# A two-layer decoder trunk: the leftover pair of the Down projection moved to its front, its seven block products regrouped, and the residual centring moved to another engine

## The chip, the cores and the metric

The kernel runs on one core of one Trainium2 chip. The metric is the device time of one execution in microseconds (us). Before the change the median of 3 runs is 2747.27 us (2745.57 to 2750.97). Engines are named as in the profile: PE is the matrix engine, PEld its weight loads, DVE the vector engine, ACT the scalar engine, POOL the GpSimd engine, SP the engine that only issues transfers.

## What is computed

The input is one sequence of 1024 tokens with 1024 channels, in float32. Layer 0 mixes tokens with a state-space scan and a short gated convolution, layer 1 with sliding-window attention. After the mixer each layer does the same:

```python
def swiglu(x, w_gate, w_up, w_down):
    return (jax.nn.silu(x @ w_gate) * (x @ w_up)) @ w_down
...
x = layer_norm(ALPHA * x + mixer(x))
x = layer_norm(ALPHA * x + swiglu(x, ...))
x = x + (p[i] @ W_ple) * sigmoid(x @ W_gate + b_gate)
```

The hidden width is 2816, that is 22 slices of 128. The last line is called the PLE gate below; `p` has 256 channels.

## The kernel before

**Data.** Activations stand transposed: `r[m]` holds 128 channels (m = 0 to 7) by 1024 tokens, and a "half" H is 512 tokens. To keep float32 accuracy every operand is split into a high part (a rounding to the matmul type, made by a conversion on ACT) and a low part (the difference, made on DVE or POOL), and each product is three matmuls of 128x128 weights by 512 columns: high by high, high by low, low by high. A result block stands in one of eight PSUM banks of 128x512.

**Gate and up.** Slices 0 and 1 of the hidden width are done plainly and written to DRAM as `hC`. The other 20 slices go in 10 pairs, q = 0 to 9. In a pair, `seven` (L358) computes a 2x2 block product with seven instead of eight block products, for gate and then for up. From the pair's four blocks of h, the seven right-hand sides of the coming Down product are formed on DVE (`c`, `n`) and written to DRAM by SP as `hT[7, pair]` (L429). POOL adds the eight row blocks of x in `token_sum` (L402), from which the mean over channels is taken and written out as `xmd`.

**Down.** `ffn` does the 10 pairs in chunks of 4, 4 and 2 (L450). In a chunk it goes through seven products B11, B21, T2, T1, T3, B22, T4 (the loop at L552); a step is one product, and a kp inside it is two pairs, that is 24 matmuls. Each step needs weight combinations `wd`, made in `w8` (L509, L145, L502, L503) from raw weights `wr` by sums and differences in `left` (L541 to L546), and h tiles: loaded by POOL (`tf`, L393), split by ACT (`tt`, L470) and DVE (L471). Products accumulate in four banks `dx` or four banks `dy`. After every step four banks are added into `rr` (the result in SBUF), by ACT copies the first time (L490) and DVE additions after that (L488). In the second chunk the residual x is read back, centred on DVE (`rx` minus `xm`, L457) and added. After the chunks comes the **plain pair** (bank `dn`): hidden slices 0 and 1, from `hC`, 96 matmuls, eight banks per half. Behind each of its banks the statistics of the norm are gathered (`norm.add`), and `norm.finish(0)` (L216 is its reciprocal) writes the first half while the products of the PLE gate's first factor (`ple_products`) run.

**Column means.** All the weights of Down are centred. The means of their columns are taken early, while the input projection of layer 0 runs: 44 units, each a load of 512 KB by POOL (`dc`, L985) and one ACT instruction (L989), with three buffers and four units asked for after each half of a column block.

**Order.** Each engine works through its own list in order. The lists are made by a scheduler at build time, so they are read from the built program. Buffers come from pools; a tile that takes the place of another waits for the other's last reader, and that reader may be a transfer to DRAM.

Of the kernel before, what the change touches and what calls it, by code (L numbers as in the profile page):

```python
# [7 lines left out]
F32 = mybir.dt.float32  # L8
# [12 lines left out]
PLAG = 6  # L21
# [21 lines left out]
def trunk(ctx: ExitStack, tc: tile.TileContext, xT, pT, w_in, w_dt, w_out, w_q, w_k, w_v, w_o, w_gate, w_up, w_down,  # L43
# [118 lines left out]
    class Norm:  # L162
# [11 lines left out]
        def square(self, H, m):  # L174
            rm = self.r[m][:, hs(H)]
            if m == 0:
                self.q[H] = self.pool.tile([P, HB], F32, tag="lnq", name="lnq", bufs=2)
                A.activation(self.q[H], rm, AF.Square)
            else:
                sq = self.pool.tile([P, HB], F32, tag="lnt", name="lnt", bufs=2)  # L180
                A.activation(sq, rm, AF.Square)
                V.tensor_add(self.q[H], self.q[H], sq)
# [80 lines left out]
    def ffn_first(layer, X, tp, norm, extra):  # L263

        hC = tc.dram_tile([2, 2, P, HB], F32, name=f"hC{layer}")
        xmd = tc.dram_tile([2, P, HB], F32, name=f"xm{layer}")
# [7 lines left out]
        return w, hC, xmd, extra  # L274

    def ffn(layer, first, X, r, X2):
        w01, hC, xmd, (wq, cq) = first
        hT = tc.dram_tile([7, NPAIR, P, HB], F32, name=f"hT{layer}")
        xs = tc.dram_tile([KT, P, NT], F32, name=f"xs{layer}")
        c1 = ExitStack()  # L280
# [117 lines left out]
        def token_sum(q):  # L398

            acc, new = xsum[:, 0], xsum[:, 1]  # L400
            if 1 < q <= KT:
                G.tensor_add(acc, acc, new)  # L402
            if q < KT:
                nc.gpsimd.dma_start(new if q else acc, xs[q])
            elif q == KT:
                for H in range(2):
                    pm = bank("a", "xm")
                    T.matmul(pm, mean, acc[:, hs(H)], start=True, stop=True)
                    A.copy(new[:, hs(H)], pm)
                nc.gpsimd.dma_start(xmd.rearrange("h p n -> p h n"), new.rearrange("p (h n) -> p h n", h=2))  # L410

        for q in range(NPAIR):
# [3 lines left out]
            with tc.high_priority():  # L416
                A.activation(g1, g1, AF.Silu)
                A.activation(g2[:, h1], g2[:, h1], AF.Silu)
                A.activation(g2[:, h0], px, AF.Silu)
            u1, u2, px = seven(weights(w_up[layer, f], w_up[layer, f + 1]), "")  # L420
            if q == NPAIR - 1:
                early = [[load_t(hT[w, i:i + 2]) for i in (0, 2)] for w in (B11, B21)]
# [9 lines left out]
            token_sum(q)  # L432
# [14 lines left out]
        wraw = pool(c2, "wraw", bufs=4)  # L447
# [6 lines left out]
        def residuals(ms, rx, xm):  # L454
            for m in ms:
                t = rx.pop(0)
                V.tensor_sub(t, t, xm)  # L457
                stt(rr[m], t, ALPHA, rr[m], ALU.mult, ALU.add)

        turn = [0]  # L460

        def t8(name):
            i = turn[0] % 6
            turn[0] += 1
            return (fe if i < 2 else ft).tile([P, 2, 2, HB], F32R, tag="t", name=name, bufs=2 if i < 2 else 4)
# [10 lines left out]
        def new(j, H):  # L476
            if j % 2 == 0:
                x8[H] = wraw.tile([P, 2, 2, HB], F32R, tag="wr", name=f"x{j}{H}") if H == 1 and j >= 4 else t8(f"x{j}{H}")
# [5 lines left out]
        def add(m, H, ps):  # L484
            o = rr[m][:, hs(H)]
            with tc.high_priority():
                if (m, H) in touched:
                    V.tensor_tensor(out=o, in0=o, in1=ps, op=ALU.add)  # L488
                else:
                    A.copy(o, ps)  # L490
            touched.add((m, H))

        for ch, (q0, n) in enumerate(chunks):
            kps = range(n // 2)

            def w8(src, name, kp, which):
# [8 lines left out]
                for i in range(2):  # L505
                    f = 2 * (q0 + 2 * kp + i) + 2
                    c = NFF + f // 2 - 1 if which == T1 else f if which == B11 else f + 1
                    c = cen[:, layer, c:c + 1]
                    A.activation(w[:, 0, i], src[:, i], AF.Identity, bias=c)  # L509
                    stt(w[:, 1, i], src[:, i], c, w[:, 0, i].bitcast(F32), ALU.add, ALU.subtract)  # L510
# [13 lines left out]
            def raw_load():  # L524
                with tc.high_priority() if ch else ExitStack():
                    v = {}
                    for j in (0, 1) if ch else (1, 0):
                        for kp in kps:
                            t = wraw.tile([P, 2, KT, P], F32, tag="wr", name="wr")
# [5 lines left out]
            def left(kp, which):  # L535
# [3 lines left out]
                if which == T2:  # L539
# [4 lines left out]
                    return a11  # L544
                if which == B22:
                    V.tensor_sub(a12, a12, a11)  # L546
                return {T1: s1s[kp], T3: a21, B22: a12, T4: a22}[which]
# [4 lines left out]
            for step, which in enumerate((B11, B21, T2, T1, T3, B22, T4)):  # L552
                into_x = step % 2 == 0
                if step in (1, 3):
                    yb = [bank("a", f"dy{p}") for p in range(4)]
                bs = xb if into_x else yb
                fresh = step in (0, 1, 3)
                for kp in kps:
                    if step == 0 or step == 1 and ch:
                        W = direct(kp, step)  # L560
                    elif step == 1:
# [6 lines left out]
                    tt = split_t(early[step][kp] if ch == 0 and step < 2 else load_t(hT[which, q:q + 2]))  # L568
                    for i in range(2):
                        kk = 2 * kp + i  # L570
                        t = tt[:, i]
                        for p in range(4):
                            for j, (l, xl) in enumerate(((0, 0), (0, 1), (1, 0))):
                                T.matmul(bs[p], W[:, l, 4 * i + p, :], t[:, xl, :], start=fresh and kk == 0 and j == 0,  # L574
                                         stop=kk == n - 1 and j == 2, skip_group_check=True)
                if ch == 1:
                    residuals([[], [0], [1], [2], [3], [4, 5], [6, 7]][step], rx, xm)
                    for m in [[0], [1], [2], [3], [4, 5], [6, 7], []][step]:
                        rx.append(f4(xpool, "rx", "x"))
                        nc.gpsimd.dma_start(rx[-1], xs[m])  # L580
                elif ch == 0 and step == 6:
                    xm = f4(xpool, "xm", "x")
                    nc.gpsimd.dma_start(xm.rearrange("p (h n) -> p h n", h=2), xmd.rearrange("h p n -> p h n"))
                for p in range(4):
                    for m, H in {B11: [(0, 0)], B21: [(0, 0)], T2: [(0, 1)], T1: [(1, 1)], T3: [(1, 1)], B22: [(0, 1)], T4: [(1, 0)]}[which]:
                        add(2 * p + m, H, bs[p])
# [738 lines left out]
```

## Time and profile before

| | us |
|---|---|
| median of 3 runs | 2747.27 (2745.57 to 2750.97) |
| the profiled execution | 2751.04 |
| its span in the trace | 2749.3 |
| PE busy | 2650.7 (96%) |
| DVE busy | 1780.2 (65%) |
| ACT busy | 1134.5 (41%) |
| POOL busy | 436.8 (16%) |

The mean granted PE clock is 0.987 of full speed. The profiled execution is 3.8 us longer than the median. Matmuls are pipelined: one shows as 0.39 us long, though the next starts 0.23 us later, so the number of matmuls in a stretch tells more than PE's busy time. Layer 0's gate and up phase with `seven` runs from about 855 to 1244 us, its Down from 1244 to about 1507; layer 1's Down begins at about 2394.

### The profile page before, as it was taken

How to read it: one execution, taken by the hardware profiler on the slowest of the kernel's cores; microseconds unless marked ns; L12 is line 12 of the kernel's file. 1: busy time of each engine (PE TensorE's matmuls, PEld its weight loads, DVE VectorE, ACT ScalarE, POOL GpSimd, SP SyncE). 2: the span in 40 equal slices, each digit the busy share in tenths (PEclk: the TensorE clock that was granted, in tenths of full speed). 3: DMA queues.
4: the chain of work that ended last, by engine and by line, in shares of the span. 5: the costliest groups of instructions: out<-in, count | busy, mean ns of one | idle time of the engine just before them, and what ended most of it. 6: DMA issues, size and time to landing. Idle time of an engine off the chain costs nothing.

```text
span 2749.3 us, 31895 instructions
## 1 busy us (share of the span) xinstructions
PE 2650.7 (96%) x12234; PEld 2134.0 (78%) x12234; DVE 1780.2 (65%) x2763; ACT 1134.5 (41%) x1824; POOL 436.8 (16%) x387
## 2 busy tenths in 40 slices
PE   8999999999998999998999999999989999989999
PEld 6777777887876888886788887777778888867887
DVE  6787522274588666555897637775976556569873
ACT  5442362241244333333445546663533333343371
POOL 1111142111214100001121221001330000111122
PEclk9999999999999999999999999999999999989999
DMA  3100272311113323246543420002243233546332
GB/s 135 39 25 30 94 267 92 115 46 46 54 46 145 130 100 114 79 156 226 187 166 114 131 85 24 16 28 96 92 142 106 82 115 109 203 182 219 107 139 92
DMA packets 108697, 300.72 MB, mean 109 GB/s; under 512 B 10320, under 2 KB 27088, under 8 KB 108544
## 3 DMA queue, kind: packets, MB, share of 16 engines
q1 hardware_dynamic: 76624, 184.37, 19.4%
q0 software_dynamic: 31920, 114.31, 11.9%
q8 instruction: 96, 1.57, 0.2%
q14 instruction: 57, 0.47, 0.1%
HBM read 233.63 MB, written 65.01 MB: 109 GB/s over the span
## 4 chain that ended last, share of the span: by engine, by line
PE 77%; DVE 10%; issue 5%; ACT 4%; DMA 3%; POOL 1%; SPq 0%; POOLq 0%; ACTq 0%; DVEq 0%
PE px L358 16%; PE g L135 8%; PE g L136 8%; PE g L134 8%; PE pz L358 8%; PE pg L693 5%; PE dx L574 5%; PE dy L574 4%; PE py L358 4%; PE o L1152 2%; DMA hT<-c 1%; DVE tt L471 1%; PE pt L1143 1%; PE yd L944 1%; POOL dc L985 1%
## 5 line engine op out<-in xcount | busy, mean ns | idle before, releaser
L134 PE MATMUL g<-x,W 128*128 128x512 f32 x992 | 398.7, 402 | 13.3 <-ACT W L129 4.9
L135 PE MATMUL g<-x,W 128*128 128x512 f32 x992 | 396.9, 400 | 4.5 <-DVE x L112 2.6
L136 PE MATMUL g<-x,W 128*128 128x512 f32 x992 | 397.0, 400 | 2.5 <-POOL W L130 2.5
L130 POOL TENSOR_TENSOR W<-st,W 128x1024 fp32r<-128x1024 f32 x63 | 153.6, 2439 | 821.9 <-ACT W L129 821.7
L574 PE MATMUL dx<-tt,wd 128*128 128x512 f32 x960 | 228.3, 396 | 12.2 <-ACT tt L470 5.1
L134 PEld LDWEIGHTS g<-x,W 128*128 128x128 f32 x992 | 189.4, 191 | 57.6 <-ACT x L111 6.3
L358 PE MATMUL px<-T,wV 128*128 128x512 f32 x960 | 230.9, 389 | 1.5 <-DVE c L368 1.5
L135 PEld LDWEIGHTS g<-x,W 128*128 128x128 f32 x992 | 189.2, 191 | 49.1 <-DVE x L112 5.4
L574 PEld LDWEIGHTS dx<-tt,wd 128*128 128x128 f32 x960 | 182.9, 191 | 54.8 <-ACT tt L470 6.0
L136 PEld LDWEIGHTS g<-x,W 128*128 128x128 f32 x992 | 189.3, 191 | 43.9 <-POOL W L130 3.6
L358 PEld LDWEIGHTS px<-T,wV 128*128 128x128 f32 x960 | 180.0, 188 | 39.6 <-DVE c L368 2.3
L574 PE MATMUL dy<-tt,wd 128*128 128x512 f32 x720 | 181.0, 409 | 19.7 <-ACT wd L509 12.1
L129 ACT CAST W<-st 128x1024 fp32r<-128x1024 f32 (+1 forms) x97 | 100.5, 1040 | 209.8 <-PE g L136 145.5
L574 PEld LDWEIGHTS dy<-tt,wd 128*128 128x128 f32 x720 | 141.2, 198 | 56.0 <-ACT wd L509 13.8
L358 PE MATMUL px<-T,wS 128*128 128x512 f32 x480 | 118.2, 396 | 13.7 <-ACT c L368 13.7
L358 PEld LDWEIGHTS px<-T,wS 128*128 128x128 f32 x480 | 91.9, 192 | 33.8 <-ACT c L368 14.6
L470 ACT CAST tt<-tf 128x1024 fp32r<-128x1024 f32 x74 | 75.8, 1046 | 101.2 <-PE dx L574 42.4
L358 PE MATMUL px<-x,wA 128*128 128x512 f32 x480 | 116.2, 391 | 0.0
L471 DVE TENSOR_TENSOR tt<-tf,tt 128x1024 fp32r<-128x1024 f32 x74 | 89.0, 1220 | 41.0 <-ACT tt L470 40.8
L358 PE MATMUL pz<-T,wU 128*128 128x512 f32 x480 | 115.3, 389 | 0.0
L358 PE MATMUL pz<-x,wS 128*128 128x512 f32 x480 | 115.3, 389 | 0.0
L358 PE MATMUL py<-x,wA 128*128 128x512 f32 x480 | 115.3, 389 | 0.0
(318 smaller groups left out, 5289.4 us busy)
## 6 DMA issues: line engine op xcount, KB each, us to landing
tf<-hT POOLq DMA_DIRECT2D x70, 512.0 KB, 4.9
dc<-in_w_down POOLq DMA_DIRECT2D x44, 512.0 KB, 4.9
st<-in_w_gate SPq DMA_DIRECT2D x44, 512.0 KB, 3.2
st<-in_w_up SPq DMA_DIRECT2D x44, 512.0 KB, 4.2
st<-in_w_in SPq DMA_DIRECT2D x43, 512.0 KB, 3.2
hT<-n SPq DMA_DIRECT2D x40, 512.0 KB, 6.4
wr<-in_w_down SPq DMA_DIRECT2D x24, 512.0 KB, 5.4
hT<-c SPq DMA_DIRECT2D x20, 512.0 KB, 4.7
```

Of the source, the lines that this page charges most:

```text
L129: A.copy(W[:, 0, ks], st[:, ks])
L130: lo_eng[k % len(lo_eng)].tensor_sub(W[:, 1, ks], st[:, ks], W[:, 0, ks].bitcast(F32))
L134: T.matmul(ps, W[:, 0, i, :], X[:, 0, :], start=first, stop=False)
L135: T.matmul(ps, W[:, 0, i, :], X[:, 1, :], start=False, stop=False)
L136: T.matmul(ps, W[:, 1, i, :], X[:, 0, :], start=False, stop=last)
L358: T.matmul(ps, W[:, l, o + k, :], x[:, xl, :], start=first and k == 0 and j == 0, stop=k == 3 and j == 2, skip_group_check=True)
L470: A.copy(t[:, :, 0], st)
L471: V.tensor_sub(t[:, :, 1], st, t[:, :, 0].bitcast(F32))
L574: T.matmul(bs[p], W[:, l, 4 * i + p, :], t[:, xl, :], start=fresh and kk == 0 and j == 0, stop=kk == n - 1 and j == 2, skip_group_check=True)
L693: T.matmul(ps[:, c:c + n], W[m][l][:, i, :], X[i][H][:, xl, c:c + n], start=i == j == 0, stop=i == KT - 1 and j == 2)
L944: T.matmul(yd[64 * k:64 * k + 64, ci * P:(ci + 1) * P], xdt[:, ci, p * P + 64 * k:p * P + 64 * k + 64], M[:, k * 256 + ci * P:k * 256 + (c ...
L1152: T.matmul(ov[64 * hd:64 * hd + 64, bi * P:(bi + 1) * P], vt[:, b - 1 + kb, vc], pt[hd][:, 2 * bi + kb, :], start=kb == kbs[0], stop=kb == 1)
```

## The change

- **Plain pair first.** It moves from the end of Down to its start. Its sixteen banks are the first to touch `rr`, so they leave by ACT copies; all later ones are DVE additions. Its `hC` tiles and the four early `hT` tiles are loaded in the last up product.
- **Two chunks instead of three**, of 4 and 6 pairs: 28 bank additions of 128x512 fewer per layer.
- **Order in the last chunk**: B11, B21, T2, T3, T4, T1, B22, with T2, T3 and T4 following each other on the same four banks. The rows of the first half of the tokens are final after T4, and `norm.finish(0)` stands inside T1. The loop over the four banks is now outside the loop over the pairs of a kp, so banks end one after another.
- **Residual.** POOL subtracts the mean in the gate and up phase and writes the centred rows out (`xc`): eight more loads, subtractions of 128x1024 and writes per layer. DVE keeps only the scaled addition, now in chunk 0.
- **PLE gate.** Its inputs and weights are loaded in step B22, and all eight `ple_products` stand behind B22. The lag between the halves (`PLAG`) is 4 instead of 6.
- **Column means**: two buffers instead of three, and up to three units per half at three places instead of four at one.

```diff
-PLAG = 6
+PLAG = 4
...
+        token = token_steps()
...
+            for k in range(KT):
+                nc.gpsimd.dma_start(new, xs[k])
+                yield
+                G.tensor_sub(new, new, acc)
+                nc.gpsimd.dma_start(xc[k], new)
...
             if q == NPAIR - 1:
-                early = [[load_t(hT[w, i:i + 2]) for i in (0, 2)] for w in (B11, B21)]
+                hh = [load_t(hC[H]) for H in range(2)]
+                early = [load_t(hT[w, i:i + 2]) for w in (B11, B21) for i in (0, 2)]
...
-        chunks = [(0, 4), (4, 4), (8, 2)]
+        chunks = [(0, 4), (4, 6)]
...
+        hh = [split_t(t) for t in hh]
+        for H in range(2):
+            for m in range(MT):
+                ps = bank("a", "dn")
+                for i in range(2):
+                    mm3(ps, Wd[i], m, hh[H][:, i], i == 0, i == 1)
+                add(m, H, ps)
...
-            for step, which in enumerate((B11, B21, T2, T1, T3, B22, T4)):
+            for step, which in enumerate((B11, B21, T2, T3, T4, T1, B22) if end else (B11, B21, T2, T1, T3, B22, T4)):
...
+                    if end and which == T1 and kp == 1:
+                        norm.finish(0)
+                    for p in range(4):
+                        for i in range(2):
...
-                residuals([[], [0], [1], [2], [3], [4, 5], [6, 7]][step], rx, xm)
+                if ch == 0:
+                    for t, m in rx:
+                        stt(rr[m], t, ALPHA, rr[m], ALU.mult, ALU.add)
...
-            cp = pool(cctx, "cen", bufs=3, side="right")
+            cp = pool(cctx, "cen", bufs=2, side="right")
...
-                for _ in range(4) if j >= 2 else ():
+                if j >= 2:
                     next(cs, None)
```

Three places in the engines' lists show the move. The first is ACT at the start of layer 0's Down. A number behind a name is a tile's own; `tt` is a split h tile, `rr` the result, `dx` and `dn` banks, `W` and `wd` weights. Before:

```order
L470 CAST tt<-tf 128x2x512 x2
L509 ACTIVATE wd<-st,vec 128x512 x2
L509 ACTIVATE wd<-wr,vec 128x512 x2
L470 CAST tt<-tf 128x2x512 x2
L509 ACTIVATE wd<-wr,vec 128x512 x2
L490 COPY rr_8515<-dx_8523 128x512
L490 COPY rr_8517<-dx_8524 128x512
L490 COPY rr_8519<-dx_8525 128x512
L490 COPY rr_8521<-dx_8526 128x512
L509 ACTIVATE wd<-wr,vec 128x512 x2
```

And with the change:

```order
L477 CAST tt<-tf 128x2x512 x2
L506 ACTIVATE W<-st,vec 128x1024
L506 ACTIVATE wd<-st,vec 128x512 x2
L500 COPY rr_8542<-dn 128x512
L500 COPY rr_8543<-dn 128x512
L500 COPY rr_8544<-dn 128x512
L477 CAST tt<-tf 128x2x512 x2
L500 COPY rr_8545<-dn 128x512
L477 CAST tt<-tf 128x2x512
L500 COPY rr_8546<-dn 128x512
L500 COPY rr_8547<-dn 128x512
L500 COPY rr_8548<-dn 128x512
```

The first four copies of the plain pair's banks now stand ahead of the h tile that comes third for the seven products (the single `tt` row), and the other twelve copies behind it.

The second place is DVE there, where `s` and `wr` are the sums of raw weights in `left`, and the scaled addition with `rx` is one residual row. Before:

```order
L145 SCALAR_TENSOR_TENSOR wd<-wr,vec,wd 128x512 x2
L471 TENSOR_TENSOR tt<-tf,tt 128x2x512 x2
L145 SCALAR_TENSOR_TENSOR wd<-wr,vec,wd 128x512 x2
L541 TENSOR_TENSOR s_8685<-wr 128x1024
L542 TENSOR_TENSOR wr<-wr 128x8x128
L543 TENSOR_TENSOR wr<-s_8685,wr 128x8x128
L541 TENSOR_TENSOR s_8723<-wr 128x1024
L546 TENSOR_TENSOR wr<-wr 128x8x128
L542 TENSOR_TENSOR wr<-wr 128x8x128
L471 TENSOR_TENSOR tt<-tf,tt 128x2x512
```

And with the change:

```order
L478 TENSOR_TENSOR tt<-tf,tt 128x2x512 x4
L574 TENSOR_TENSOR s_8861<-wr 128x1024
L574 TENSOR_TENSOR s_8865<-wr 128x1024
L575 TENSOR_TENSOR wr<-wr 128x8x128 x2
L576 TENSOR_TENSOR wr<-s_8861,wr 128x8x128
L576 TENSOR_TENSOR wr<-s_8865,wr 128x8x128
L145 SCALAR_TENSOR_TENSOR rr_8543<-rx,rr_8543 128x1024
L145 SCALAR_TENSOR_TENSOR wd<-st,vec,wd 128x512 x2
L145 SCALAR_TENSOR_TENSOR wd<-wr,vec,wd 128x512
```

Four splits, six raw sums and a residual row now stand in one piece ahead of the low parts of the second weight tile of B11 (`wd<-st`).

The third place is ACT in the input projection, where `c` is the first column block of a half and `dc` a unit of the column means. Before:

```order
L1006 COPY c<-g 128x512
L989 ACTIVATE dc,vec<-dc 128x1024 x3
L129 CAST W<-st 128x1024
L1010 ACTIVATE ysc_2623<-spre,vec 128x512
L989 ACTIVATE dc,vec<-dc 128x1024 x3
L129 CAST W<-st 128x1024
L989 ACTIVATE dc,vec<-dc 128x1024 x3
L1006 COPY c<-g 128x512
```

And with the change:

```order
L1034 COPY c<-g 128x512
L1017 ACTIVATE dc,vec<-dc 128x1024 x2
L129 CAST W<-st 128x1024
L1042 ACTIVATE ysc_2623<-spre,vec 128x512
L1017 ACTIVATE dc,vec<-dc 128x1024 x2
L129 CAST W<-st 128x1024
L1017 ACTIVATE dc,vec<-dc 128x1024 x2
L1034 COPY c<-g 128x512
```

Between two copies `c` stood nine units and now stand six; over all, the 44 units lie in five halves before (8, 9, 10, 8, 9) and in seven now (6, 6, 8, 6, 8, 6, 4).

## Rows read from the trace of the kernel before

**Rows 1.** The page, busy time: engine, us, share of the span, instructions.
```profile
PE 2650.7 (96%) x12234; PEld 2134.0 (78%) x12234; DVE 1780.2 (65%) x2763; ACT 1134.5 (41%) x1824; POOL 436.8 (16%) x387
```

**Rows 2.** Windows: length, then busy us (instructions) per engine, PEclk, DMA share, GB/s.
```profile
930.00:1080.00 150.00, 150.00 (x664) 124.20 (x663) 90.67 (x115) 51.70 (x68) 0.00 (x0) 1.00 0.31 106
1250.00:1400.00 150.00, 134.84 (x552) 107.19 (x551) 112.51 (x124) 62.02 (x80) 23.41 (x35) 0.94 0.60 211
2400.00:2550.00 150.00, 134.25 (x542) 106.44 (x541) 114.54 (x126) 62.38 (x81) 23.20 (x34) 0.93 0.59 207
```

**Rows 3.** Waits of PE in layer 0's Down: us in total, times, longest.
```profile
PE dy L574 <- ACT wd L509: 6.3, 2, 4.0
PE dy L574 <- DVE wd L145: 2.7, 2, 1.8
PE dx L574 <- ACT tt L470: 2.6, 1, 2.6
```

**Rows 4.** Timeline of PE, first products of layer 0's Down: start, us, count, idle before.
```profile
1244.25 11.04 PE L574 MATMUL dx<-tt,wd 128*128 128x512 f32 x48
1255.13 5.60 PE L574 MATMUL dy<-tt,wd 128*128 128x512 f32 x24
1264.70 8.63 PE L574 MATMUL dy<-tt,wd 128*128 128x512 f32 x24 [3.97 <-ACT wd L509]
```

**Rows 5.** Timeline of ACT, same place: third conversion of an h tile.
```profile
1262.98 1.04 ACT L470 CAST tt<-tf 128x1024 fp32r<-128x1024 f32 x1 [16.25 <-DMA hT<-c]
```

**Rows 6.** DMA, 1225 to 1275: queues (packets, MB, share), then issues to landing.
```profile
q0 software_dynamic: 2448, 8.91, 48.7%
q1 hardware_dynamic: 5184, 3.93, 24.3%
...
tf<-hT POOLq DMA_DIRECT2D x9, 512.0 KB, 11.0
wr<-in_w_down POOLq DMA_DIRECT2D x8, 512.0 KB, 5.8
...
hT<-c SPq DMA_DIRECT2D x1, 256.0 KB, 17.3
```

**Rows 7.** Windows, six microseconds after the last up product.
```profile
1250.00:1256.00 6.00, 6.00 (x28) 4.99 (x27) 0.63 (x1) 0.00 (x0) 0.72 (x1) 1.00 1.04 395
```

**Rows 8.** Groups of DVE in layer 0's Down: count, busy, mean ns, idle.
```profile
L471 DVE TENSOR_TENSOR tt<-tf,tt 128x1024 fp32r<-128x1024 f32 x35 | 42.1, 1219 | 15.9 <-ACT tt L470 15.8
L488 DVE TENSOR_TENSOR rr<-rr,dx 128x512 f32<-128x512 f32 x36 | 23.4, 683 | 3.1 <-PE dx L574 3.1
...
L145 DVE SCALAR_TENSOR_TENSOR wd<-wr,vec,wd 128x512 fp32r<-128x512 f32 x24 | 17.3, 745 | 0.1
...
L457 DVE TENSOR_TENSOR rx<-rx,xm 128x1024 f32<-128x1024 f32 x8 | 9.5, 1218 | 0.0
```

**Rows 9.** Timeline of POOL and DVE, one such sum and DVE beside it.
```profile
899.98 2.61 POOL L402 TENSOR_TENSOR xsum<-xsum 128x1024 f32<-128x1024 f32 x1 [2.96 <-DMA xsum<-xs]
...
900.84 2.29 DVE L434 TENSOR_TENSOR n<-c 128x512 f32<-128x512 f32 x1
```

**Rows 10.** Windows, the stretch of all seven sums.
```profile
865.00:911.00 46.00, 45.36 (x194) 37.11 (x195) 31.71 (x34) 14.54 (x20) 20.92 (x13) 0.97 0.54 180
```

**Rows 11.** Windows, 100 us in which the column means are taken.
```profile
350.00:450.00 100.00, 92.56 (x395) 74.34 (x394) 24.29 (x39) 50.85 (x85) 35.42 (x38) 0.98 0.63 213
```

**Rows 12.** Windows of the column means' ACT instructions alone (two a unit), 100 us.
```profile
325.00:425.00 100.00, 49.63 (x87) 0.98 0.76 258
```

**Rows 13.** Timeline of ACT there: one column mean and its wait.
```profile
368.07 1.06 ACT L989 ACTIVATE dc<-dc 128x1024 f32<-128x1024 f32 x1 [3.58 <-DMA dc<-in_w_down]
```

**Rows 14.** The page, DMA issues: KB each, median us to landing.
```profile
dc<-in_w_down POOLq DMA_DIRECT2D x44, 512.0 KB, 4.9
```

**Rows 15.** Timeline of DVE, end of layer 0's Down and the norm behind it.
```profile
1505.28 1.30 DVE L488 TENSOR_TENSOR rr<-rr,dn 128x512 f32<-128x512 f32 x2
...
1538.93 0.69 DVE L112 TENSOR_TENSOR x<-rr,x 128x512 fp32r<-128x512 f32 x1
```

More of the change, by code (lines that the diff above doesn't have):

```diff
@@ L567, in ffn @@
                     q = q0 + 2 * kp
[L568 to L572, printed above, removed]
+                    tt = split_t(early.pop(0) if early else load_t(hT[which, q:q + 2]))
+                    if end and kp == kps[-1] and which in (T4, T1):
+                        w = {T4: T1, T1: B22}[which]
+                        early = [load_t(hT[w, q0 + 2 * i:q0 + 2 * i + 2]) for i in kps]
@@ L584, in ffn @@
+                e, H = reads[which]
                 for p in range(4):
-                    for m, H in {B11: [(0, 0)], B21: [(0, 0)], T2: [(0, 1)], T1: [(1, 1)], T3: [(1, 1)], B22: [(0, 1)], T4: [(1, 0)]}[which]:
-                        add(2 * p + m, H, bs[p])
-        loaded = ple_load(layer, wraw, t8)
-        hh = [split_t(load_t(hC[H])) for H in range(2)]
+                    add(2 * p + e, H, bs[p], end and which in (B21, T4, T1, B22))
         lo_eng[:] = [V]
-        Wd = []
-        for i in range(2):
-            with tc.high_priority():
-                st = spool.tile([P, KT, P], F32, tag="st", name="st")
-                nc.sync.dma_start(st, w_down[layer, i])
-                W = wpool.tile([P, 2, KT, P], F32R, tag="w", name="W")
-                c = cen[:, layer, i:i + 1]
-                A.activation(W[:, 0], st, AF.Identity, bias=c)
-                stt(W[:, 1], st, c, W[:, 0].bitcast(F32), ALU.add, ALU.subtract)
-            Wd.append(W)
@@ L602, in ffn @@
-        for H in range(2):
-            for m in range(MT):
-                ps = bank("a", "dn")
-                for i in range(2):
-                    mm3(ps, Wd[i], m, hh[H][:, i], i == 0, i == 1)
-                add(m, H, ps)
-                with tc.high_priority() if H == 0 else ExitStack():
-                    norm.add(H, m)
-            if H == 0:
-                ple_products(layer, *loaded, range(4))
-                norm.finish(0)
-                ple_products(layer, *loaded, range(4, MT))
-                wpools[:] = [wpool] * 3 + [As(wraw, "wr")] * 2
@@ L615, in ffn @@
-        return rr, c2, lnp, norm
+        wpools[:] = [wpool]
+        ple_products(layer, PX, Wp, range(MT))
+        return rr, c2, lnp, norm, As(wraw, "wr")
     class As:
@@ L674, in pieces, with weight @@
             return hi, lo
-        for m in range(4):
-            W[m] = pieces(m)
+        def weight(m):
+            if m in (3, 4):
+                W[m] = pieces(m)
+            else:
+                w = unit(w_pg[layer, m], at=more if m in (5, 6) else None)
+                W[m] = w[:, 0], w[:, 1]
+        for m in range(6):
+            weight(m)
         for m, H in lag_order(MT, PLAG):
@@ L680, in ple @@
                 norm.finish(1)
-            if H == 0 and m >= 4:
-                w = unit(w_pg[layer, m])
-                W[m] = w[:, 0], w[:, 1]
+            if H == 0 and 5 <= m < MT - 1:
+                weight(m + 1)
             pw = tp.tile([P, HB], F32, tag="pw", name="pwt", bufs=2)
@@ L1019, in trunk @@
         lo_eng[:] = [V, G]
+        for _ in cs:
+            pass
         cctx.close()
```

160 lines of the change are left out of this document (94 added, 66 removed).

## The prediction

> **What bounds the kernel now.** I read the busy times first. PE is busy 96% of the span, DVE 65% [rows 1], and the change leaves the number of matmuls as it is, so time can come only from stretches where PE does not run at its rate. I look for these in the windows. In a steady stretch 664 matmuls start in 150 us, 0.226 us each [rows 2]; that is the rate to measure against. In the first 150 us of layer 0's Down only 552 start: 112 are missing, 25.3 us. In layer 1's it is 542: 122 are missing, 27.6 us. So 52.9 us of the 2751.0 are lost at the start of the two Downs, which is what the change rebuilds.
>
> The waits of PE in layer 0's Down say for what: high parts of weights from ACT 6.3 us, low parts from DVE 2.7 us, the conversion of h tiles on ACT 2.6 us [rows 3]. PE's timeline has the place. It starts Down at 1244.25 and does 72 matmuls, then waits 3.97 us, and the 24 matmuls behind that wait take 8.63 us [rows 4], where 24 at the steady rate take 5.4: PE came back at its lower clock, 1.2 instead of 2.4 GHz, after the pause. ACT's timeline names the cause. The third conversion stood 16.25 us, until 1262.98, for the write `hT<-c` [rows 5]: its tile lies where that write still reads. And the write is late because of traffic: 256 KB took 17.3 us to land, while nine loads `tf` and eight `wr` of 512 KB were on the way [rows 6] and the transfer engines moved 395 GB/s at a share of 1.04 [rows 7], which is all they give here. So the last writes of h share the transfers with the first loads of Down, and PE has 72 matmuls, 16.3 us, to bridge that.
>
> **The change part by part.**
>
> *Plain pair first.* Its 96 matmuls are 21.8 us of PE work that need neither `hT` nor raw weights. The work is moved, not added; at its old place nothing waited on it. What it covers is the late write. But the write is still in the way: ACT's new list has four bank copies, then the conversion that waits for `hT<-c`, then the other copies. With eight banks and four emptied, PE can do 12 banks of 6 matmuls, 16.3 us. The write was issued about 1.3 us after the start of Down and takes 17.3 [rows 5, 6], so the conversion ends near 19.6 and PE stands up to 3.4 us. If the write lands as fast as the small loads (5.8 us) it stands 0. Ends 0 and 3.4; I take **2.0**, nearer to the row of the same transfer. The pause is then shorter than the 3.97 us after which PE fell to the lower clock.
>
> How fast such a write goes can be asked of the Trainium skill too: by its page "DMA: Bandwidth & Descriptors", section "Queues, rings and completion order", each transfer engine goes round between the queues it has work for, a packet at a time. With packets of 3.6 KB on POOL's queue and 0.76 KB on SP's (MB over packets), SP's queue would get 17% of 395 GB/s, an estimate of 68 GB/s; the 768 KB of both `c` writes [rows 6] would take 11.5 us and the stall be nil, which makes the total 4 us lower. The row has 17.3, and the row goes into the sum.
>
> *Behind it on DVE.* Four splits, six raw sums and a residual row now precede the low parts of B11's second weight tile. The last split can start when its conversion ends, at 19.6; it takes 1.22, the six sums and the residual 7 x 1.22, the two low parts 2 x 0.75 [rows 8], which gives 30.9. PE wants them after 21.8 + 5.4 + 2.0 = 29.2. Stall **1.6** (0 if the sums run while DVE waits for that split, 4 with another microsecond or two of transfer).
>
> *Chunk 0.* Its DVE list holds 14 splits (17.1), 28 low parts in 14 weight tiles (about 19), 8 raw sums (9.8), 8 residual rows (9.7) and 28 bank additions (19.1) [rows 8]: some 75 us beside 14 x 24 matmuls, 76 us. That fits, but the list is in order, and today DVE's low parts cost 2.7 us in a Down that is less full. **1.5** (0 to 4).
>
> *Fewer bank additions, centring away.* 28 additions of 0.683 and 8 subtractions of 1.218 per layer leave DVE, 28.9 us [rows 8]. They lie beside PE work, so they pay only by making room for the two terms above; I count nothing for them again. Behind the six-pair chunk's boundary and where T2, T3 and T4 follow each other on the same banks, a bank is free for an addition 1.36 us ahead of the next, and an addition takes 0.68. **1.5** (0 to 3).
>
> *Norm and last step.* `finish(0)` stands after one kp of T1, and the reciprocal and the sums of squares wait for the last additions of T4; in step B22 the conversions for the PLE gate stand ahead of one h tile. By the lengths on DVE and POOL (0.7 to 2.6 us each) [rows 8, 9], **2.3** (0 to 5).
>
> *PLE gate.* From the last bank addition (1506.58) to the last split of the second half (1539.62) pass 33 us [rows 15]. All `ple_products`, 21.8 us, and five products of 5.4 us now lie between: 49 us, enough for a lag of 4. **0.5** (0 to 2).
>
> So a Down would lose 2.0 + 1.6 + 1.5 + 1.5 + 2.3 + 0.5 = 9.4 us, both 18.8, against 52.9: a **gain of 34.1**. With all the low ends 0 is lost and with all the high ends 21.4 in each.
>
> *Centring on POOL.* Eight more subtractions per layer, near the sums' 2.61 us [rows 9], and 16 transfers of 512 KB, lie in gate and up, where PE runs full and transfers at a share of 0.31 [rows 2]. They are paced by pairs some 65 us apart. Nothing. What covers them is the 40% of DVE that is idle there: beside such a sum, a DVE subtraction took 2.29 us [rows 9] instead of 0.68. The Trainium skill, page "SBUF — State Buffer", section "SBUF: two separate sides", has the rule: DVE and POOL share one port pair, and whoever comes second waits out the other's whole instruction. The row agrees, and the rule speaks against this move; I price it as a rival.
>
> *Column means.* In the 100 us concerned 395 matmuls start [rows 11] of 442: 47 missing, 10.6 us. With three buffers nearly all of the 88 instructions of the 44 units lie in 100 us [rows 12], some 2.2 us a unit, 98 in all, against 81 us of PE work in their five halves (72 matmuls each): 17 us more, of which 10.6 show and banks bridge some 7. Two buffers give, per unit, half of (load + 1.06 + about 0.5 of turning round); with a load of 3.6 [rows 13] that is 2.6 us, with the median 4.9 [rows 14] 3.2 us. Over seven halves, 114 us of PE work, 44 units take 114 to 142 us, and banks bridge 7 again. The loss is thus 0 to 21 instead of 10.6: a gain of 10.6 or a loss of 10. Fewer loads at once should make each faster, so I lean to the lower end: a **gain of 3**.
>
> **Sum.** 2751.0 − 34.1 − 3 = 2713.9 for the profiled execution. The median lies 3.8 below that, and I keep **2714** for it, leaving those 4 us for waits that I did not find.
>
> **Rivals.**
>
> *The stall moves behind the pair.* If the write lands 5 us later than today, since two `hC` tiles are loaded as well, PE stands over 6 us, comes back at the lower clock (3.2 us for 24 matmuls) [rows 4], and DVE's list is as late: some 9 more per layer, **2732**. For it: the transfers are full [rows 7]. Against: `hC` is loaded a product earlier. 0.16.
>
> *Nearly all stalls go.* DVE's room swallows them: 4 lost per layer and 8 gained in the means, 2751 − 45 − 8 = **2698**. For it: the 28.9 us per layer. Against: in-order lists always leave some. 0.14.
>
> *POOL holds DVE up.* If each of 16 subtractions delays DVE by 1.6 us, as the sum in the row does [rows 9], and PE feels each, 26 us go, **2740**. Against: beside seven sums PE was busy 45.36 of 46 us [rows 10]. 0.04.
>
> *Slower: the column means become the bound.* With a unit at u us the loss is 44u − 121. It eats all of Down's gain when it passes 10.6 + 34, at u = 3.8, that is a load of 6 us with two under way. At 4.1 the loss is 59 and the time about **2762**. Against: the median load is 4.9 with three under way. 0.07.
>
> **How the numbers follow.** The forecast has 0.59, with its own bounds 2704 to 2724. Range 2697 to 2740: it leaves out the slower case and the tails of the others, some 0.15 to 0.2. A difference of 0.2%, 5.5 us, is about what a measurement can tell from none. Faster by more: forecast, both milder rivals and most of the POOL case, 0.88; within: 0.05; slower: 0.07.
>
> **What would show it.** In the windows of the changed kernel the first 150 us of each Down should hold 620 to 660 matmuls; in PE's timeline the pair should run 72 matmuls without a gap, then pause under 3.5 us, and no 24 matmuls behind take 8 us. In ACT's timeline the third h tile's conversion should still wait for `hT<-c`. Waits of PE for the means' copies should be fewer. I am wrong if either Down loses over 16 us, if the stretch of the means loses more than 15, or if gate and up fall below 664 matmuls in 150 us.

## The result and the profile after

The changed kernel takes 2716.47 us (median of 4 runs, 2714.06 to 2721.06), the kernel before 2749.12 beside it. The ratio is 0.9877, with a 95% interval of 0.9846 to 0.9908: 1.2% faster. The forecast of 2714 is 2.5 us off. The profiled execution's span fell by 37.1 us, from 2749.3 to 2712.2, and the sum had 37.1. But the parts do not match: several terms of the sum were wrong, and their errors cancel.

The busy times of the changed kernel answer to [rows 1]. POOL is busy 60 us more. DVE has 72 instructions less, 57.7 us at the lengths of [rows 8], yet it is busy only 18.7 us less: some 39 us went into other instructions that got longer.

```profile
PE 2636.0 (97%) x12234; PEld 2128.4 (78%) x12234; DVE 1761.5 (65%) x2691; ACT 1133.7 (42%) x1824; POOL 496.9 (18%) x431
```

The windows of the changed kernel (length, busy us and instructions per engine, PEclk, DMA share, GB/s) answer to [rows 2, 11]:

```profile
350.00:450.00 100.00, 93.91 (x398) 76.20 (x397) 21.95 (x38) 52.57 (x89) 37.76 (x43) 0.97 0.67 233
930.00:1080.00 150.00, 150.00 (x660) 123.50 (x659) 93.19 (x114) 51.28 (x68) 11.06 (x8) 1.00 0.35 123
1250.00:1400.00 150.00, 150.00 (x664) 124.20 (x663) 125.07 (x145) 68.01 (x90) 25.34 (x37) 1.00 0.65 227
1400.00:1500.00 100.00, 95.57 (x408) 77.32 (x407) 65.50 (x71) 58.02 (x83) 26.80 (x22) 0.98 0.32 112
2400.00:2550.00 150.00, 150.00 (x664) 124.20 (x663) 120.43 (x145) 63.58 (x81) 21.73 (x31) 1.00 0.52 178
2550.00:2650.00 100.00, 94.51 (x402) 76.14 (x401) 75.18 (x76) 63.59 (x92) 35.32 (x32) 0.98 0.36 126
```

Both Downs now begin at the full rate: 664 matmuls in the first 150 us, where 552 and 542 were [rows 2]. At 0.226 us each that gives 52.9 us back, all that was lost there. Gate and up hold 660, with eight POOL instructions that were not there. The four that are missing (0.9 us) are no loss to POOL: the mean's own four matmuls `xm` now stand in this window (1051.14), the only place in it where matmuls start late; before they stood at 1204.40, outside it. The column means have not improved: 398 matmuls, 395 before [rows 11]. And a new loss stands at the end of Down: 408 and 402 matmuls in the last 100 us. The same two windows of the kernel before:

```profile
1400.00:1500.00 100.00, 98.99 (x435) 81.27 (x434) 78.50 (x102) 48.78 (x70) 23.28 (x20) 1.00 0.29 103
2550.00:2650.00 100.00, 100.00 (x441) 82.44 (x440) 77.91 (x102) 50.40 (x73) 23.69 (x20) 1.00 0.28 99
```

That is 27 and 39 fewer, 14.9 us. So 52.9 − 14.9 = 38.0 us come from Down and next to nothing from elsewhere. PE's waits in layer 0's Down and the gate behind it (us in total, times, longest) name the new place; the three kinds of wait in [rows 3] had 11.6 us:

```profile
PE dy L619 <- DVE tt L478: 3.5, 2, 2.2
PE pg L721 <- DVE x L112: 1.2, 1, 1.2
PE dy L619 <- ACT tt L477: 1.0, 1, 1.0
```

How the start was emptied shows in four places of the changed kernel. SP's timeline, POOL's, ACT's, and the DMA issues between 1215 and 1265 us (KB each, us to landing):

```profile
1242.76 0.34 SPq L438 DMA_DIRECT2D hT<-c  x1
...
1245.27 0.72 SPq L438 DMA_DIRECT2D hT<-c  x1
```

```profile
1243.77 3.13 POOL L564 DMA_DIRECT2D wr<-in_w_down  x6 [6.39 <-PE px L358]
```

```profile
1250.44 1.06 ACT L477 CAST tt<-tf 128x1024 fp32r<-128x1024 f32 x1
```

```profile
hT<-c SPq DMA_DIRECT2D x1, 512.0 KB, 14.3
hT<-c SPq DMA_DIRECT2D x1, 256.0 KB, 2.0
```

The first write `hT<-c` goes out 1.0 us ahead of the last six raw loads and lands in 2.0 us. The same two issues before, of SP and POOL:

```profile
1245.60 1.58 SPq L429 DMA_DIRECT2D hT<-c  x2
```

```profile
1242.67 3.13 POOL L531 DMA_DIRECT2D wr<-in_w_down  x6 [4.33 <-PE px L358]
```

There the write went out three microseconds behind the first of those six loads and took 17.3 [rows 6]. Both ends moved: against the start of Down the write goes out 1.9 us earlier and the six loads 2.0 us later. The second write goes out behind them and takes 14.3. The third conversion of an h tile, which stood 16.25 us [rows 5], starts at 1250.44 without any wait. The chain behind it on DVE is early too; its low parts for B11's second pair:

```profile
1265.35 1.42 DVE L145 SCALAR_TENSOR_TENSOR wd<-st,vec,wd 128x512 fp32r<-128x512 f32 x2 [0.22 <-ACT wd L506]
```

They end at 1266.8, 23.5 us after the pair's first matmul (1243.31), and PE wants them after 27.2. That is what the pair covers here: without its 21.8 us PE would want these low parts after 5.4.

The new loss is in step B22 of the last chunk, 7.4 us in each layer: 4.5 are the waits for `tt` above, most of the rest is PE behind them (the granted clock of the window is 0.98). The changed kernel's timeline of POOL and DVE there (start, us, line, tile):

```profile
1439.82 6.20 POOL L656 TENSOR_TENSOR p<-st,p 128x1024 fp32r<-128x1024 f32 x2
...
1452.73 2.45 POOL L667 TENSOR_TENSOR wp<-st,wp 128x1024 fp32r<-128x1024 f32 x1 [2.23 <-PE dy L619]
```

```profile
1443.69 3.42 DVE L478 TENSOR_TENSOR tt<-tf,tt 128x1024 fp32r<-128x1024 f32 x1
...
1448.16 2.88 DVE L182 TENSOR_TENSOR lnq<-lnq,lnt 128x512 f32<-128x512 f32 x1
...
1453.63 2.64 DVE L478 TENSOR_TENSOR tt<-tf,tt 128x1024 fp32r<-128x1024 f32 x1
```

POOL makes the low parts of the PLE gate's inputs `p` in one piece from 1439.82 to 1446.0. A split on DVE that falls into it takes 3.42 us, a sum of squares 2.88 beside the next one, another split 2.64 beside the last. A split takes 1.22 us elsewhere [rows 8], such a sum 0.68 in the same timeline (1452.29). The Trainium skill, page "SBUF — State Buffer", section "SBUF: two separate sides", says that DVE and POOL share a port pair which one instruction holds to its end; these rows agree.

### The profile page after: what moved, and what is told of

Read it like the earlier page. It is cut to its first block, busy times and chain, and to the rows that moved or that the text cites. A ratio compares the mean times of both kernels' runs of the same rounds, so it can differ in the third digit from the quotient of the medians.

```text
span 2712.2 us, 31793 instructions
## 1 busy us (share of the span) xinstructions
PE 2636.0 (97%) x12234; PEld 2128.4 (78%) x12234; DVE 1761.5 (65%) x2691; ACT 1133.7 (42%) x1824; POOL 496.9 (18%) x431
## 4 chain that ended last, share of the span: by engine, by line
PE 82%; DVE 9%; issue 4%; ACT 2%; POOL 1%; DMA 1%; SPq 0%; POOLq 0%; ACTq 0%; DVEq 0%
PE px L358 16%; PE g L135 8%; PE g L136 8%; PE g L134 8%; PE dx L619 8%; PE pz L358 8%; PE pg L721 5%; PE dy L619 5%; PE py L358 4%; PE o L1186 2%; DVE x L112 1%; PE pt L1177 1%; DVE lnq L182 1%; PE yd L972 1%; PE yo L978 1%
## 5 line engine op out<-in xcount | busy, mean ns | idle before, releaser
L619 PE MATMUL dx<-tt,wd 128*128 128x512 f32 x960 | 219.2, 389 | 0.0
L619 PE MATMUL dy<-tt,wd 128*128 128x512 f32 x720 | 171.1, 397 | 8.8 <-DVE tt L478 6.9
L721 PE MATMUL pg<-x,W 128*128 128x512 f32 (+1 forms) x600 | 133.9, 383 | 2.9 <-DVE x L112 2.3
L721 PEld LDWEIGHTS pg<-x,W 128*128 128x128 f32 x600 | 109.4, 188 | 26.3 <-DVE x L112 3.1
L478 DVE TENSOR_TENSOR tt<-tf,tt 128x1024 fp32r<-128x1024 f32 x74 | 97.3, 1320 | 30.6 <-ACT tt L477 23.9
```

The lines of the kernel that those rows point to most:

```text
L478: V.tensor_sub(t[:, :, 1], st, t[:, :, 0].bitcast(F32))
L619: T.matmul(bs[p], W[:, l, 4 * i + p, :], tt[:, i, xl, :], start=fresh and kk == 0 and j == 0, stop=kk == n - 1 and j == 2, skip_group_chec ...
L721: T.matmul(ps[:, c:c + n], W[m][l][:, i, :], X[i][H][:, xl, c:c + n], start=i == j == 0, stop=i == KT - 1 and j == 2)
```

## The experiments

The prediction's theory was: the pair covers a write that stays late; stalls of a few microseconds remain behind it on ACT and DVE; the room on DVE helps. The rivals: the write is no longer late, because of where it is issued; or the room on DVE is what counts. For the end of Down: POOL holds DVE up, or the order on ACT and SP does.

**1. The pair alone.** On the kernel before:

```diff
             if q == NPAIR - 1:
+                hh = [load_t(hC[H]) for H in range(2)]
...
+        hh = [split_t(t) for t in hh]
+        for H in range(2):
+            for m in range(MT):
+                ...
+                add(m, H, ps)
...
+        ple_products(layer, *loaded, range(MT))
+        norm.finish(0)
```

Expected:

> The kernel before with one edit: the plain pair at the start of Down; three chunks, their order, the centring on DVE and the column means stay. If moving the pair is what empties the start of Down, the first 150 us of both Downs hold 640 or more matmuls (552 and 542 before) and the time falls to 2705 to 2730, less what the end of Down gives back, since no products of the pair lie over the first half's norm any more. If the room on DVE (fewer additions, no centring) is what empties it, the first 150 us stay under 610 and the time above 2735.

Measured: 2740.39 us, ratio 0.9963 (0.9949 to 0.9978). Its windows, and PE's wait at the end of layer 0's Down:

```profile
1250.00:1400.00 150.00, 146.59 (x636) 120.75 (x635) 126.47 (x145) 64.50 (x84) 24.65 (x36) 0.98 0.64 221
1400.00:1500.00 100.00, 88.58 (x386) 72.11 (x384) 75.01 (x96) 50.21 (x70) 20.74 (x18) 0.96 0.33 116
2400.00:2550.00 150.00, 146.11 (x637) 120.17 (x636) 126.26 (x146) 61.67 (x78) 25.35 (x37) 0.99 0.59 206
2550.00:2650.00 100.00, 86.38 (x362) 69.25 (x361) 73.92 (x96) 53.17 (x76) 21.70 (x18) 0.93 0.33 116
```

```profile
PE pg L693 <- ACT x L111: 11.1, 1, 11.1
```

The start is nearly emptied, 636 and 637 matmuls, though DVE still makes all additions and the centring: 179 matmuls more than before, 40.5 us. The end gives 29 of them back (386 and 362 against 435 and 441). PE waits 11.1 us for the first half's rows, since the pair and the products between its halves had been the cover of that norm. So moving the pair is worth its full price only with a new order of the last chunk. And this run does not test the pair against a late write, for the write was not late here either. It went out at 1245.68, landed in 5.4 us, and the third conversion (1253.36) did not wait for it:

```profile
hT<-c SPq DMA_DIRECT2D x1, 256.0 KB, 5.4
```

My range missed the total by 10 us: I had the price of the end too low.

**2. The write alone.** The kernel before, the pair at its old place:

```diff
+            with tc.high_priority() if q == NPAIR - 1 else ExitStack():
+                V.tensor_tensor(out=u2[:, h1], ...)
+                V.tensor_tensor(out=u1, ...)
             def keep(t, at, n=2):
-                nc.sync.dma_start(
+                with tc.high_priority() if q == NPAIR - 1 else ExitStack():
+                    nc.sync.dma_start(
```

Expected:

> The kernel before with the last pair's sums and writes of h put first in the scheduler's order; the pair stays at the end. If the lateness of the write is a matter of issue order (in the changed kernel it landed in 2.0 us, issued 1 us ahead of the raw loads, before in 17.3 us, issued 3 us behind the first of them), it now lands in under 10 us, the third conversion waits under 8 us and each Down loses at most 17 instead of 25 us in its first 150 us: 2730 to 2738. If the write is late because the transfers are full whatever the order, it still takes 14 us or more and the time stays within 4 us of before.

Measured: 2728.29 us, ratio 0.9923 (0.9899 to 0.9946). Its windows, the landing of the first write, and ACT's third conversion:

```profile
1250.00:1400.00 150.00, 137.90 (x586) 110.98 (x585) 121.49 (x135) 67.23 (x87) 25.38 (x37) 0.98 0.62 221
2400.00:2550.00 150.00, 140.00 (x591) 113.18 (x590) 125.54 (x140) 65.79 (x84) 25.37 (x37) 0.97 0.59 207
```

```profile
hT<-c SPq DMA_DIRECT2D x1, 256.0 KB, 7.2
```

```profile
1253.14 1.05 ACT L472 CAST tt<-tf 128x1024 fp32r<-128x1024 f32 x1 [5.57 <-DMA hT<-c]
```

An edit of the order alone, without moving any product, brings 21 of the 33 us. The write lands in 7.2 us instead of 17.3, the conversion waits 5.57 instead of 16.25, and the first 150 us hold 586 and 591 matmuls. What is still lost there, some 17 us in each layer, is gone in the changed kernel and for the most part in run 1, where the pair stands first; PE waits most for low parts of weights:

```profile
PE dy L576 <- DVE wd L145: 4.0, 2, 2.2
```

**3. The write late again.** The changed kernel, with two DVE passes that change nothing between the last h blocks and their writes, which now also stand behind the sums `n`:

```diff
+            if q == NPAIR - 1:
+                V.tensor_tensor(out=u2, in0=u2, in1=u2, op=ALU.max)
+                V.tensor_tensor(out=u1[:, h0], in0=u1[:, h0], in1=u1[:, h0], op=ALU.max)
+                keep(u2, B21)
+                keep(u1[:, h0], B11, 1)
```

Expected:

> The changed kernel with 1.9 us of idle DVE passes over the last h blocks ahead of their writes, so that the writes are issued behind the raw loads as before. If the pair's 21.8 us are cover enough by themselves, PE loses under 3 us per Down at the start and the time is 2714 to 2723. If what decides is that the write goes out ahead of the loads, it lands 15 us or more after its issue, ACT stands at the fifth bank copy, PE waits after 12 banks and comes back at the lower clock: 5 to 10 us per Down, 2726 to 2738.

Measured: 2718.83 us, ratio 0.9886 (0.9865 to 0.9908), the same as the changed kernel. SP's issue of the write, ACT's conversion that waits for it, and the window:

```profile
1253.42 2.62 SPq L438 DMA_DIRECT2D hT<-c  x1
```

```profile
1263.77 1.05 ACT L483 CAST tt<-tf 128x1024 fp32r<-128x1024 f32 x1 [4.03 <-DMA hT<-c]
```

```profile
1250.00:1400.00 150.00, 149.04 (x658) 123.06 (x657) 125.01 (x145) 69.15 (x91) 24.66 (x36) 1.00 0.66 231
```

The write goes out at 1253.42, ACT stands 4.03 us until it has landed, 19.5 us after the pair's first matmul (1244.26), and PE starts 658 matmuls of 664 all the same. So in this build the pair is cover enough for the late write, as the prediction had it. But my waiting fifth copy did not occur: here the conversion stands behind ten of the sixteen copies, not four, so what a late write costs in the order of the changed kernel is not shown. In the changed kernel itself this cover was not called on.

**4. Three chunks.** The changed kernel:

```diff
-        chunks = [(0, 4), (4, 6)]
+        chunks = [(0, 4), (4, 2), (6, 4)]
```

Expected:

> The changed kernel with chunks of 4, 2 and 4 pairs instead of 4 and 6: 28 additions of 128x512 more on DVE per layer, 19 us. If the room on DVE decides, Down loses 5 to 15 us more per layer, 2726 to 2745. If DVE has room to spare, 2714 to 2722.

Measured: 2729.08 us, ratio 0.9929 (0.9909 to 0.9949). PE's waits between 1430 and 1480 us, and the window of the start:

```profile
PE pw L679 <- ACT wp L666: 9.8, 1, 9.8
PE pw L681 <- POOL wp L667: 1.3, 1, 1.3
```

```profile
1250.00:1400.00 150.00, 150.00 (x663) 124.25 (x662) 136.02 (x165) 66.57 (x87) 27.51 (x42) 1.00 0.66 233
```

The total is what the room on DVE would have given, the place is not: with 28 additions more the start still holds 663 matmuls. The 13 us go at the end, where step B22 has 48 matmuls instead of 72 and no longer covers the loads and conversions of the gate's weights (these loads go out at 1463.93, some 4 us after the step's last product): 11.1 us of waits for `wp`, where the changed kernel has 4.5 of other waits in that step. In this run the long last chunk is worth its cover, not its missing additions.

**5. Centring on DVE again.** The changed kernel:

```diff
-                nc.gpsimd.dma_start(new, xs[k])
-                yield
-                G.tensor_sub(new, new, acc)
-                nc.gpsimd.dma_start(xc[k], new)
...
+                        V.tensor_sub(t, t, xm)
                         stt(rr[m], t, ALPHA, rr[m], ALU.mult, ALU.add)
```

Expected:

> The changed kernel with the centring back on DVE: 8 subtractions of 128x1024 (9.7 us) per layer in chunk 0, POOL's eight subtractions, loads and writes gone. If DVE is as full in chunk 0 as the prediction had it (75 of 76 us), PE loses 5 to 9 us more per Down: 2726 to 2735, and the first 150 us fall from 664 to under 645 matmuls. If DVE has room there (125 of 150 us busy in the changed kernel), 2713 to 2720 and 655 or more matmuls.

Measured: 2723.96 us, ratio 0.9893 (0.9879 to 0.9908). PE's waits in layer 0's start, and DVE's second sum of raw weights ahead of the low parts:

```profile
PE dx L618 <- DVE wd L145: 2.7, 1, 2.7
```

```profile
1270.40 1.23 DVE L570 TENSOR_TENSOR s<-wr 128x1024 f32<-128x1024 f32 x1 [9.00 <-DMA hT<-n]
```

Both Downs start with 649 and 650 matmuls: 14 fewer, 3 us in each, one wait of 2.7 us for low parts of weights. That is between the two expectations, and for another reason than either: DVE is not full, it stands 9.00 us for a write `hT<-n` that landed late (8.83 in layer 1). Behind that wait come the sums and one subtraction of 1.22 us, and the low parts end 31.1 us after the pair's first matmul instead of 23.5. The place is the one that the second step of the prediction named; the 1.22 us of centring alone do not explain 3 us.

**6. The column means.** The changed kernel, with three buffers and four units in one place, as before (`bufs=3`, and the three `next(cs, None)` back to one loop of four). Expected:

> The changed kernel with the column means as before: three buffers, four units in one place per half. If two buffers and three places are worth the 3 us of the prediction, the time rises by 2 to 5 us, to 2718 to 2722, and 350 to 450 us hold fewer matmuls than the 398 of the changed kernel, near 390. If the loads through ACT's list cost the same either way (395 before, 398 now), the time stays within 2 us of the changed kernel.

Measured: 2713.66 us, ratio 0.9857 (0.984 to 0.9873), 407 matmuls in 350 to 450 us. The changed kernel once more, on the chip of the last two runs:

> The changed kernel once more, unaltered, on the same chip as the two runs behind it, for the comparison: 0.986 to 0.990 of the kernel before, 398 matmuls in 350 to 450 us.

Measured: 2714.64 us, ratio 0.9866 (0.9849 to 0.9882), 396 matmuls. The two intervals overlap: the form of the means is without effect that can be measured, and a gain of 3 us does not show.

**7. Low parts of the gate on DVE, and a control.** The changed kernel:

```diff
-                    PX = ple_inputs(layer, wr)
-                    Wp = ple_weights(layer)
+                    with tc.high_priority():
+                        PX = ple_inputs(layer, wr)
+                        Wp = ple_weights(layer)
...
-            G.tensor_sub(t[:, 1], sv, t[:, 0].bitcast(F32))
+            V.tensor_sub(t[:, 1], sv, t[:, 0].bitcast(F32))
...
-            G.tensor_sub(t[1], st, t[0].bitcast(F32))
+            V.tensor_sub(t[1], st, t[0].bitcast(F32))
```

The control has the first part of it only (`high_priority`). Expected:

> The changed kernel with the low parts of the PLE gate's inputs and weights made on DVE instead of POOL, and put first in the scheduler's order. In step B22 of the changed kernel two splits on DVE took 3.42 and 2.64 us beside POOL's subtractions instead of 1.22, and PE lost about 7 us per Down there. If POOL holding DVE up is the cause, these splits take 1.3 us, B22 loses under 3 us per Down and the time falls to 2704 to 2711. If the cause is the conversions for the gate that stand ahead of h tiles on ACT and their loads, DVE's four extra subtractions change nothing or cost more: 2714 to 2722.

> The changed kernel with the PLE gate's inputs and weights put first in the scheduler's order, POOL still making the low parts: the control of the run before. If POOL's subtractions beside DVE are the cause of the loss in B22, it stays at 6 us or more per Down and the time at 2713 to 2720. If the order on ACT and SP is the cause, it falls to 2704 to 2711 as with DVE.

Measured: 2704.90 us on DVE, ratio 0.9822 (0.9808 to 0.9837); 2718.83 us for the control, ratio 0.9876 (0.9861 to 0.989). The timeline of DVE in the first, then of POOL and DVE in the control, and the end of Down in the first:

```profile
1446.68 1.21 DVE L478 TENSOR_TENSOR tt<-tf,tt 128x1024 fp32r<-128x1024 f32 x1
...
1451.82 1.21 DVE L478 TENSOR_TENSOR tt<-tf,tt 128x1024 fp32r<-128x1024 f32 x1
```

```profile
1445.73 6.21 POOL L657 TENSOR_TENSOR p<-st,p 128x1024 fp32r<-128x1024 f32 x2
```

```profile
1449.61 3.42 DVE L478 TENSOR_TENSOR tt<-tf,tt 128x1024 fp32r<-128x1024 f32 x1
```

```profile
1400.00:1500.00 100.00, 100.00 (x439) 82.04 (x438) 67.02 (x78) 60.95 (x86) 14.91 (x19) 1.00 0.35 121
```

With the subtractions on DVE the splits take 1.21 us, 439 matmuls start where 408 did, and 13.9 us separate the two runs. On POOL a split takes 3.42 and the loss stays (411 matmuls). So it is the move of the four subtractions that removes the loss, and the first of PE's waits there, 1.3 us, is for the split of 3.42.

But the control does not hold the order on ACT fixed. Its ACT list in this stage is the one of the changed kernel; the build with the subtractions on DVE has another. ACT's timeline in that build, then in the control:

```profile
1450.32 1.06 ACT L477 CAST tt<-tf 128x1024 fp32r<-128x1024 f32 x1 [2.38 <-PE dy L620]
...
1455.14 1.05 ACT L667 CAST wp<-st 128x1024 fp32r<-128x1024 f32 x1 [1.74 <-DMA st<-in_w_p]
```

```profile
1457.00 0.63 ACT L181 ACTIVATE lnt<-rr 128x512 f32<-128x512 f32 x1 [3.41 <-DVE lnq L182]
1457.54 1.03 ACT L667 CAST wp<-st 128x1024 fp32r<-128x1024 f32 x1
1458.48 1.04 ACT L477 CAST tt<-tf 128x1024 fp32r<-128x1024 f32 x1
```

In the first the last h tile is converted ahead of both `wp`, in the control behind them and behind a wait of 3.41 us for the sum of squares that DVE finishes late. Had it stood behind the second `wp` in the first too (1455.14), it would have come after PE began the last 24 matmuls of the step (1455.6, worked out from their end at 1461.00). So POOL's hold on DVE is shown for the first wait; for the other two, 3.2 us and what follows them, hold and order act together, and no run separates them.

**8. Both edits, and a fourth buffer.** The kernel with low parts on DVE and the means of run 6, then the same with

```diff
-            cp = pool(cctx, "cen", bufs=3, side="right")
+            cp = pool(cctx, "cen", bufs=4, side="right")
```

and one more load under way. Expected:

> The changed kernel with the PLE gate's low parts on DVE (first in order) and the column means as before (three buffers, one place). If both effects are separate, step B22 loses under 1 us, 350 to 450 us hold some 407 matmuls, and the time is 10 to 16 us under the changed kernel, 0.980 to 0.983 of the kernel before. If the means' form is without effect, as far as a run can tell, it is the same as with the low parts alone, 0.982 to 0.983.

> As the run before, with four buffers and three loads under way for the column means. If the number of loads under way is what ACT waits for (two: 398 matmuls in 350 to 450 us, three: 395 to 407), four give 410 or more and 2 to 5 us less than three. If the transfers are full there, more loads under way land later each, and neither the matmuls nor the time change by more than 2 us.

Measured: 2703.52 us, ratio 0.9827 (0.9812 to 0.9841), and 2690.39 us, ratio 0.9777 (0.9763 to 0.9792). The groups of the means' ACT instructions between 300 and 450 us, for the changed kernel (two buffers), three and four (count, busy, mean ns, idle before), and the window of four:

```profile
L1017 ACT ACTIVATE dc<-dc 128x1024 f32<-128x1024 f32 x43 | 45.6, 1061 | 60.6 <-DMA dc<-in_w_down 60.4
```

```profile
L1018 ACT ACTIVATE dc<-dc 128x1024 f32<-128x1024 f32 x44 | 46.6, 1060 | 39.8 <-DMA dc<-in_w_down 38.6
```

```profile
L1018 ACT ACTIVATE dc<-dc 128x1024 f32<-128x1024 f32 x44 | 46.6, 1059 | 24.5 <-DMA dc<-in_w_down 22.4
```

```profile
350.00:450.00 100.00, 100.00 (x443) 82.81 (x442) 27.41 (x42) 53.16 (x87) 39.04 (x40) 1.00 0.58 215
```

ACT stands for these loads 60, 39 and 22 us. With 1.06 + 0.18 us of work and all idle time before it a unit costs 2.7, 2.1 and 1.8 us. ACT's list asks for 6.3 units in a half with two buffers (44 in seven halves) and 8.8 with three or four (44 in five): 16.7, 18.9 and 15.8 us, beside 16.3 us of PE work. Only the last is under it, and only there does PE run at its rate, 443 matmuls. That this is why the third buffer brings nothing and the fourth all is worked out from these rows, not tried by itself; with two buffers an average of 0.4 us too much in each of seven halves does not account for the 44 matmuls (10 us) that are missing. This is worth 13 us, and this last kernel is 2.2% faster than the one before and 0.9% faster than the changed one (0.9777 against 0.9866).

## Why the prediction came out right, step by step

- **Where the time lay**: right. The 52.9 us at the start of both Downs are what came back.
- **The pair's cover, 2.0 us of stall** (0 to 3.4): measured 0, for a reason that I had not seen. I took the landing of 17.3 us over from the row, though the change also moves the write: it now leaves 1.0 us ahead of six raw loads. I had read the order of ACT and DVE, not the times at which SP and POOL issue. Run 2 shows that an early write alone gives most of the gain; run 3 that with the pair a late one costs nothing that can be measured, in a list where the conversion stands behind ten copies. What the pair covers in the changed kernel is the chain on DVE behind that conversion.
- **The weighed rule**: the Trainium skill's page "DMA: Bandwidth & Descriptors", section "Queues, rings and completion order", gave an estimate of 11.5 us for both writes beside a full queue. Measured beside one: 17.3 before, 14.3 for the second write of the changed kernel. The first write met no full queue and took 2.0. The measurements decide: the moment of issue counted for more than the shares.
- **DVE behind it, 1.6, and chunk 0, 1.5**: measured 0. The mechanism is real (run 5 finds the wait for low parts when a late write holds DVE, at 31.1 us, where my sum had 30.9), but without the late conversion the low parts end 23.5 us into Down instead of the 30.9 of my sum, ahead of PE.
- **Boundary and same banks, 1.5**: measured 0 in the windows up to 1400 and 2550 us.
- **Norm and last step, 2.3** (0 to 5): the term that was mis-sized. The windows show 14.9 us for the two layers, 7.5 each. I had named the conversion that stands behind the gate's and priced it by POOL's own lengths, but not what POOL does to DVE beside it, nor that ACT then waits for DVE. How the 7.5 divide between that hold and the order on ACT stays open.
- **The rival that POOL holds DVE up** had a chance of 0.04, in gate and up. There PE lost nothing to it, though by the letter my sign for it came (660 matmuls in 150 us, under 664): the mean's own matmuls are the difference. Nor are the subtractions paced 65 us apart, as I wrote: in layer 0 all eight lie between 1053.73 and 1131.9, some 10 us apart. The same mechanism struck in step B22, where I did not look for it: the four subtractions were on POOL before the change too, but cost PE little there (435 and 441 matmuls). The two runs under 7 show it, as far as said there.
- **PLE gate, 0.5**: measured one wait of 1.2 us.
- **Room on DVE**: 28.9 us per layer were to go. The instructions went, but DVE's busy time fell by 9.3 per layer, and nothing in the sum hung on it.
- **Column means, a gain of 3**: measured none. A unit took 2.7 us with two buffers, near the low end that I leaned to (2.6); what failed is the step from there to the loss, 44 units less 114 us of PE work and 7 of banks, which gave none. PE's waits for the copies did not get fewer either (two of 3.6 us in all, before two of 3.7). Why 10 us are still lost is open. The number of matmuls there varied from 382 to 407 between profiles of two and three buffers.
- **The sum**: 18.8 us of losses forecast in the two Downs, about 17 found (34.7 matmuls missing at the end of one and 40.7 of the other against 442.7), of which the start has none. Per Down the terms up to the last step were 6.6 us too high and the last step 5.2 too low, and the means were 3 us too good: 13.2 − 10.4 − 3 comes to nothing. The right total is luck in its parts; the rival "nearly all stalls go" was right on the start. There the signs that I had named came better than stated: 664 matmuls where I had 620 to 660, no pause behind the first 72, and no conversion waiting for `hT<-c`.

## What to carry to other kernels

When a stall hangs on a late transfer, look up at which moment it is issued, on which queue and behind which others, both before and after the change: the order of issue alone was worth 21 us here, without moving any product. When a stage gets tighter, ask again of each operation left on POOL which DVE instructions fall beside it. When a control is built, read the lists again: an edit that looks like one change can move others. And when work is taken from the end, name what it covered there.

## What the hardware showed that I had not expected

A write of 256 KB took between 2.0 and 17.3 us in five builds of this kernel, beside six loads of 512 KB on another queue: 2.0 when it went out 1.0 us ahead of the first of them, 5.4, 7.2 and 17.3 when it went out 1.0, 1.7 and 2.9 us behind it, and 10.2 at 8.7 us behind it (run 3). Beside POOL subtractions of 128x1024 a DVE instruction of 1.22 us lasted 3.42. And ACT's waits for 512 KB loads fell steadily with two, three and four buffers (60, 39, 22 us), while PE got nothing that can be measured from the third, and with the fourth the 13 us of run 8.
